# WKV recurrence on one core: a store piece issued by GpSimd from pair 42, VectorE rounding three of four k tiles, a ring of eleven, and new places in the order

## The chip, the core and the metric

The kernel runs on one core of a Trainium2 chip. Its engines work side by side, each in the order of its own queue: TensorE (PE, with its weight loads as PEld), VectorE (DVE), ScalarE (ACT), GpSimd (POOL) and SyncE (SP, which here only issues DMAs). The metric is the device time of one execution in microseconds (us). Differences within 0.3% are the ordinary spread of one kernel's runs.

## The reference

The inputs k and v are 16 batches of 2048 steps with 256 channels, float32; w and u have 256 channels. Per batch and channel a numerator, a denominator and their common exponent are carried along the 2048 steps:

```python
for t in range(seq_len):
    ww = u + kk
    qq = np.maximum(pp, ww)
    e1, e2 = np.exp(pp - qq), np.exp(ww - qq)
    output[b, t, :] = (e1 * aa + e2 * vv) / (e1 * bb + e2 + 1e-08)
    ww = pp - w + kk
    qq = np.maximum(ww, kk)
    e1, e2 = np.exp(ww - qq), np.exp(kk - qq)
    aa, bb, pp = e1 * aa + e2 * vv, e1 * bb + e2, qq
```

So the weight of an earlier step is the exponential of a running sum over k and w, and an output is a weighted sum of v over a sum of weights.

## The kernel before

**Tiling.** Time is cut into 16 chunks of 128 steps (time on the partitions), each of two halves of 64. A unit of work, called a pair here as in the words of the change, is n = 4c + p: chunk c of four batches, a tile of 128 x 1024. There are 64 pairs, with 512 KB of k, of v and of output each.

**One pair, front part.** `load_k` and `load_v` fetch k and v. TensorE needs k in a rounded float32 form. `how(n)` says who makes it: "C", the load converts while it moves the bytes, into the pool `kpool` (NK = 4 buffers); "D" or "P", the load is plain, into `kppool` (NKP = 1 buffer, tile `kf`), and `round_k` (L184) copies it on VectorE or GpSimd into a `kpool` buffer. From pair CF = 18 on the pattern PLAN "DCPC" is read by n modulo 4; before that it is "C", apart from the first BYSP = 1 pair, whose k and v are loaded by SP into `vpool` buffers and whose k VectorE rounds. All other loads are issued by GpSimd. Twice for each pair (q = 0 and 1), `rows` (R, four matmuls, L191) and `logs` (L, two matmuls, L197) build logarithms of weights in one of two PSUM tiles X, and `exps` (L200) exponentiates them on ScalarE into the ring EZR, which has RING = 12 slots. `cast_v` (CV, L204) makes v bfloat16, on VectorE for the first EARLY = 13 pairs and then on GpSimd, and `times_v` (TV, L209) multiplies it by the weights on VectorE. `sums` (S, L235) adds up halves on TensorE.

**One chunk, state.** After the last pair of a chunk a chain of small steps carries the state: CS (copy, VectorE), TU (turn, TensorE, L248), SL (logs, ScalarE), FR, OF (VectorE), SW (ScalarE), CH, SS (VectorE), TK (turn back, TensorE, L292) and BK (copy back, VectorE, L296).

**One pair, back part,** some LAG = 10 pairs later: DEN (twelve matmuls, L312, into an X tile), LN and INV on ScalarE (L320, L324: the reciprocal by logarithm and exponential, tile `rd`), NUM (twelve matmuls, L312, into the only `num` buffer), MUL (L332, VectorE, into one of NOT = 9 output tiles `ot`), and `store` (ST), a DMA for two batches and two half-size pieces for the other two. All three are issued by SP, but from pair BYPOOL = 52 on the third piece is issued by GpSimd.

**The order.** Nothing is moved at run time: each step has a place, a number in units of a pair (n plus an offset from the table P; for the back part n + LAG plus an offset; in the last ten pairs by the table TAIL). A list planner at the end takes, again and again, the step with the lowest place whose predecessors are taken and whose buffer is free by its count, and appends it to the program. Each engine then runs its own steps in that order and waits for data and buffers as they come.

**Fillers.** Before a step with a mode, the planner puts `zeros(m)`: m matmuls of zeros, 192 columns wide, into the PSUM tile TURN (L139). The number comes from P["Z0"] for pair or chunk 0 and from P["Z"] for all others; none are put between a TK and its BK, since both use TURN:

```python
        if o["mode"] and not quiet:
            zeros(P["Z0" if name[-1] < FILL else "Z"].get(name[0], 0))
        quiet = quiet and name[0] != "BK" or name[0] == "TK"
```

Before the change, Z has 3 zeros ahead of each TK and 5 ahead of each TU, none elsewhere.

Of the kernel before, what the change touches and what calls it, by code (L numbers as in the profile page):

```python
# [15 lines left out]
def kernel(  # L16
# [9 lines left out]
    K = tc.keep_in_program_order  # L26
    PE, DVE, SC, POOL, SP = nc.tensor, nc.vector, nc.scalar, nc.gpsimd, nc.sync

    B, T, Dm = k.shape
    HS = 64  # L30
    TC = 2 * HS
    NST = T // TC
    D = 2 * Dm
    NP = 4 * NST
    RING = 12
    LAG = 10.0
    BYSP = 1
    EARLY = 13
    PLAN = "DCPC"
    NK, NKP, NV, NVB, NRD, NOT = 4, 1, 5, 2, 2, 9  # L40
    RS = 2.0 ** -20
    CAP = 54.0
    BIG = 1e30
    CF = 18
    BYPOOL = 52
    FILL = 1
    P = {"LK": -3.78, "LV": -3.8, "RK": [-0.86, -0.8, -0.88, 0.32], "L": [-8.29, -9.105],
         "X": [-13.61, -10.365], "CV": [-1.2, -1.47, -0.325, -3.63], "TV": [-0.725, 2.11, 2.53, 2.655],
         "S": [3.82, -0.625, 3.55, -2.98], "wu": -1.11, "mats": -12.33,
         "STATE": [[-8.99, -10.35, -0.28, 1.3, -0.57, 0.74, -7.0, -3.75, 3.31, 8.1, 3.65, 2.26], [3.48, 0.85, -12.96, 4.2, -4.25, -19.41, 5.21, 2.49, 5.83, -18.64, -27.57, -14.52], [-4.09, -0.42, 5.79, 1.96, 4.88, 8.33, 12.29, 3.26, 16.8, 4.18, 4.62, 9.89]],  # L50
         "R": [-0.14, -5.32],
         "OUT": {"DEN": [0.405, 0.23, 0.63, 0.44], "LN": [-0.38, -1.93, -1.0, 0.545], "INV": [-19.65, -20.535, -21.555, -15.26], "NUM": [0.92, -10.27, -1.22, -3.96], "MUL": [2.175, 2.125, 1.96, 2.125], "ST": [-7.545, -4.04, -1.22, 5.625]},
         "TAIL": {"DEN": -3.02, "LN": -3.59, "INV": 2.66, "NUM": 1.08, "MUL": -6.56, "ST": 24.12, "step": 2.857},
         "Z0": {"L": 2, "S": 0, "DEN": 16, "NUM": 8, "TK": 32, "TU": 7, "R": 15},
         "Z": {"DEN": 0, "L": 0, "NUM": 0, "TK": 3, "S": 0, "TU": 5, "R": 0}}
# [21 lines left out]
    def matrix(name, dt):  # L77
        return consts.tile([128, 128], dt, tag=name, name=name)
# [24 lines left out]
    def load_v(n):  # L103
        vr = raw(vpool, "vr")
        K((SP if n < BYSP else POOL).dma_start(out=vr, in_=rows_of(v, n)))  # L105
        VR[n] = vr
# [15 lines left out]
    Z = consts.tile([128, 192], BF16, tag="Z", name="Z")  # L122
# [14 lines left out]
    def zeros(m, first=False):  # L137
        for j in range(m):
            K(PE.matmul(TURN[:, 0:192], Z[:, 0:128], Z, start=first, stop=True, skip_group_check=True))  # L139
# [28 lines left out]
    mats = {name: matrix(name, BF16) for name in ("Id", "IdN", "S", "SN")}  # L168
# [33 lines left out]
    def cast_v(n):  # L202
        vb = vbpool.tile([128, 4, Dm], BF16, tag="vb", name="vb")
        K((DVE if n < EARLY else POOL).tensor_copy(vb, VR.pop(n)))  # L204
        VB[n] = vb
# [94 lines left out]
    RD, NUM, OT = {}, {}, {}  # L300
# [29 lines left out]
    def mult(n):  # L330
        o = opool.tile([128, 4, Dm], F32, tag="ot", name="ot")
        K(DVE.tensor_mul(o.rearrange("p (i n) d -> p i (n d)", i=2), NUM.pop(n), RD.pop(n)))  # L332
# [12 lines left out]
    ops, free = {}, {"K": NK, "KP": NKP, "V": NV, "N": 1, "RD": NRD, "OT": NOT, "VB": NVB}
# [1 line left out]
    def step(name, place, fn, args=(), after=(), take=None, give=(), mode=0):  # L347
        ops[name] = dict(place=place, fn=fn, args=args, after=list(after), take=take, give=give, mode=mode)

    for n in range(NP):  # L350
        c, j = divmod(n, 4)
        early = n < BYSP
        put = lambda key: n + P[key][j]
        m = n + LAG
        tail = n >= NP - LAG
        place = lambda key: m + (P["TAIL"][key] + (n - NP + LAG) * P["TAIL"]["step"] if tail else P["OUT"][key][j])
        kb = "V" if early else "KP" if how(n) != "C" else "K"
        if n:
# [12 lines left out]
        step(("TV", n), put("TV"), times_v, (n,), [("X", 1, n), ("CV", n), ("TV", n - 1)], None, ["VB"])  # L371
        step(("S", n), put("S"), sums, (n,), [("TV", n), ("S", n - 1)] + ([("CS", c - 1)] if j == 0 else []), mode=2)
        if j == 3:
            s = P["STATE"][0 if c == 0 else 2 if c == NST - 1 else 1]
            for i, (name, fn, *after) in enumerate((
                    ("CS", copy_sums, ("S", n)), ("TU", turn, ("CS", c), ("CH", c - 1)), ("SL", state_logs, ("TU", c)),
                    ("FR", state_frames, ("SL", c), ("SN", c - 1)), ("OF", state_offsets, ("FR", c)),
                    ("SW", state_weights, ("OF", c)), ("CH", state_chain, ("SW", c), ("KP", c - 1)),
                    ("SS", state_spread, ("CH", c)), ("TK", turn_back, ("SS", c), "mats"), ("BK", copy_back, ("TK", c)),
                    ("SN", state_next, ("OF", c)), ("KP", state_keep, ("CH", c)))):  # L380
                if not (name in ("SN", "KP") and c + 1 == NST):
                    step((name, c), n + s[i], fn, (c,), after, mode=1)
# [70 lines left out]
```

## Time and profile before

| what | value |
|---|---|
| median of 3 runs | 302.77 us (302.64 to 303.08) |
| the profiled execution | 303.64 us, of which the span from first to last instruction is 301.9 us |
| mean granted TensorE clock | 0.991 of full speed |
| bytes moved by DMA | 101.21 MB, mean 335 GB/s |

The span is what the views of the profile show; 1.74 us of the profiled execution lie around it. "Busy" is the time in which an engine has an instruction at work; an instruction's start is recorded, the end of a matmul is modelled, so for TensorE the distance from start to start is read, not the busy time. In a timeline a line has the start, the length, the engine, the source line, the operation with output and input, and how many instructions of that kind follow each other (x4). In brackets stands the idle time of the engine before it, with what ended it.

### The profile page before, as it was taken

Reading aid. Unit: us, or ns where it says so; the run is one execution under the profiler, and the core shown is the slowest. Engines: PE = TensorE matmul, PEld = TensorE weight load, DVE = VectorE, ACT = ScalarE, POOL = GpSimd, SP = SyncE. Lnnn points to the kernel's source line nnn. Section 1 sums busy time; section 2 is a strip of 40 time slices with the busy share of each in tenths; the row PEclk is TensorE's granted clock in tenths of the full one; section 3 lists DMA queues with packets and bytes.
Section 4 is the critical chain, followed back from the end, with each engine's and each line's share of the span. In section 5 each row is a group of like instructions: output and inputs, shape, how many; then the busy total and the mean of one; then the engine's idle time right before and its main releaser. Section 6 shows DMA issues by size and latency. Waiting matters only on the chain.

```text
span 301.9 us, 7960 instructions
## 1 busy us (share of the span) xinstructions
PE 279.1 (92%) x3194; PEld 140.6 (47%) x3194; DVE 238.5 (79%) x395; ACT 260.2 (86%) x289; POOL 172.7 (57%) x217
## 2 busy tenths in 40 slices
PE   7989989999999999999899999999899999996851
PEld 7536444444544454544445454445345444443420
DVE  6466865978889888977988888887988878978752
ACT  1585678999999999999899999999799997995990
POOL 8464452739577376857657576857666485521321
PEclk9999999999999999999999999999999999999996
DMA  7999999999999999999999999999999999964786
GB/s 177 339 344 348 347 350 347 329 366 314 373 375 367 374 378 353 382 377 372 347 371 371 371 380 379 382 378 370 353 357 370 372 367 346 340 172 128 229 242 171
DMA packets 69302, 101.21 MB, mean 335 GB/s; under 512 B 5128, under 2 KB 57872, under 8 KB 69264
## 3 DMA queue, kind: packets, MB, share of 16 engines
q0 software_dynamic: 34080, 67.64, 73.5%
q1 hardware_dynamic: 35168, 33.04, 35.3%
q8 instruction: 25, 0.41, 0.6%
q14 instruction: 13, 0.11, 0.1%
q10 hardware_dynamic: 16, 0.01, 0.0%
HBM read 67.12 MB, written 33.55 MB: 333 GB/s over the span
## 4 chain that ended last, share of the span: by engine, by line
PE 33%; DMA 31%; issue 13%; POOL 12%; DVE 7%; ACT 2%; POOLq 0%; DVEq 0%
DMA kf<-in_k_dram 26%; PE X L197 9%; PE num L312 6%; PE TURN L139 5%; PE X L312 5%; PE X L191 5%; DMA vr<-in_v_dram 4%; POOL kr L184 3%; DVE ot L332 3%; POOL vr L105 3%; DVE kr L184 2%; POOL kr L101 2%; PE TOT L235 2%; POOL vb L204 1%; PE TOT L248 1%
## 5 line engine op out<-in xcount | busy, mean ns | idle before, releaser
L200 ACT ACTIVATE EZR<-X 128x1024 bf16<-128x1024 f32 x128 | 124.2, 1015 | 12.5 <-PE X L197 12.5
L209 DVE TENSOR_TENSOR EZR<-EZR,vb 128x2048 bf16<-128x2048 bf16 x64 | 91.3, 1443 | 12.8 <-POOL vb L204 10.8
L332 DVE TENSOR_TENSOR ot<-num,rd 128x1024 f32<-128x1024 f32 x64 | 77.8, 1215 | 10.0 <-PE X L312 3.1
L204 POOL CAST vb<-vr 128x1024 bf16<-128x1024 f32 x51 | 53.8, 1076 | 40.4 <-DVE EZR L209 38.7
L320 ACT ACTIVATE rd<-X 128x1024 f32<-128x1024 f32 x64 | 65.4, 1022 | 5.8 <-PE X L312 2.1
L324 ACT ACTIVATE rd<-rd 128x1024 f32<-128x1024 f32 x64 | 67.8, 1059 | 2.0
L191 PE MATMUL X<-WU,CO 64*64 64x512 bf16 x512 | 52.5, 399 | 0.7
L105 POOL DMA_DIRECT2D vr<-in_v_dram x63 | 48.5, 769 | 1.5 <-issue 1.0
L197 PE MATMUL X<-kr,NLE 128*128 128x512 f32 x128 | 46.9, 448 | 0.8 <-DMA kr<-in_k_dram 0.8
L197 PE MATMUL X<-kr,NLZ 128*128 128x512 f32 x128 | 46.8, 447 | 0.0
L101 POOL DMA_DIRECT2D kr<-in_k_dram x40 | 30.5, 763 | 25.7 <-PE X L197 25.7
L312 PE MATMUL num<-EZR,SN 64*64 64x512 bf16 x256 | 26.2, 398 | 11.4 <-DVE ot L332 11.3
L191 PEld LDWEIGHTS <-CO 64*64 64x64 bf16 x512 | 15.5, 103 | 34.6 <-issue 31.1
L139 PE MATMUL TURN<-Z 128*128 128x192 bf16 x250 | 29.3, 262 | 1.6 <-DVE Z L123 1.6
L139 PEld LDWEIGHTS <-Z 128*128 128x128 bf16 x250 | 20.8, 104 | 15.5 <-issue 13.6
L312 PE MATMUL X<-EZR,S 64*64 64x512 bf16 x256 | 25.4, 380 | 0.9 <-ACT EZR L200 0.5
L197 PEld LDWEIGHTS X<-kr,NLE 128*128 128x128 f32 x128 | 19.0, 188 | 15.3 <-issue 12.9
L197 PEld LDWEIGHTS X<-kr,NLZ 128*128 128x128 f32 x128 | 19.0, 188 | 14.3 <-issue 14.3
L98 POOL DMA_DIRECT2D kf<-in_k_dram x23 | 17.5, 759 | 14.4 <-DVE U L257 9.3
L312 PE MATMUL X<-cb,Id 64*64 64x512 bf16 x256 | 25.3, 376 | 0.0
L312 PE MATMUL X<-EZR,Id 64*64 64x512 bf16 x256 | 25.3, 376 | 0.0
L312 PE MATMUL num<-cb,IdN 64*64 64x512 bf16 x256 | 25.1, 376 | 0.0
(63 smaller groups left out, 259.5 us busy)
## 6 DMA issues: line engine op xcount, KB each, us to landing
vr<-in_v_dram POOLq DMA_DIRECT2D x63, 512.0 KB, 9.5
kr<-in_k_dram POOLq DMA_DIRECT2D x40, 512.0 KB, 9.6
out_dram<-ot SPq DMA_DIRECT2D x64, 256.0 KB, 6.8
out_dram<-ot SPq DMA_DIRECT2D x116, 128.0 KB, 7.5
kf<-in_k_dram POOLq DMA_DIRECT2D x23, 512.0 KB, 6.9
out_dram<-ot POOLq DMA_DIRECT2D x12, 128.0 KB, 3.0
vr<-in_k_dram SPq DMA_DIRECT2D x1, 512.0 KB, 4.3
vr<-in_v_dram SPq DMA_DIRECT2D x1, 512.0 KB, 5.3
```

The source lines that it names most:

```text
L101: K(POOL.dma_start(out=KR[n], in_=rows_of(k, n)))
L105: K((SP if n < BYSP else POOL).dma_start(out=vr, in_=rows_of(v, n)))
L139: K(PE.matmul(TURN[:, 0:192], Z[:, 0:128], Z, start=first, stop=True, skip_group_check=True))
L191: K(PE.matmul(X[a][o:o + HS, i, :].rearrange("p (n d) -> p n d", n=2), CO[r:r + HS, q, :], WU[r:r + HS, :].unsqueeze(1).broadcast_to([HS, ...
L197: K(PE.matmul(X[a][:, i, :], (NLE, NLZ)[q], km[:, i, :], start=False, stop=True, skip_group_check=True))
L200: K(SC.activation(ez(n)[:, q, 1], X[a], ACT.Exp))
L204: K((DVE if n < EARLY else POOL).tensor_copy(vb, VR.pop(n)))
L209: K(DVE.tensor_mul(ez(n)[:, :, 0], ez(n)[:, :, 1], vb.unsqueeze(1).broadcast_to([128, 2, 2, D])))
L312: K(PE.matmul(out_tile[o:o + HS, i, :], left, right, start=s == 0, stop=s == 2, tile_position=(r, o), skip_group_check=True))
L320: K(SC.activation(rd, X[a], ACT.Ln, scale=RS))
L324: K(SC.activation(RD[n], RD[n], ACT.Exp, scale=-1.0))
L332: K(DVE.tensor_mul(o.rearrange("p (i n) d -> p i (n d)", i=2), NUM.pop(n), RD.pop(n)))
```

## The change

It changes several numbers and one function. RING 12 to 11; NKP 1 to 4 and NOT 9 to 8; BYSP 1 to 5 (the k and v of five pairs are loaded by SP, all into `vpool`, and VectorE rounds their k); EARLY 13 to 9; from pair CF = 11 on the pattern is "CDDD", so one of four k is converted by its load and three are rounded by VectorE, none by GpSimd. The third piece of a store becomes a step of its own, SQ, issued by GpSimd where `shared(n)` holds. With BYQ "PPPP", BYF = 42 and BYPOOL = 52 this is from pair 42 on (the words given with the change say 34; the code says 42). The output tile then comes free, by the planner's count, at SQ. All places are new, and so are the fillers: one zero ahead of every L, 6 ahead of TK, 7 ahead of TU. SOON = 0 makes `lead` zero, so the two terms with it change nothing.

```diff
-    RING = 12
+    RING = 11
     LAG = 10.0
-    BYSP = 1
-    EARLY = 13
-    PLAN = "DCPC"
-    NK, NKP, NV, NVB, NRD, NOT = 4, 1, 5, 2, 2, 9
+    SOON = 0
+    UNTIL = 32
+    SHARE = 0.8
+    BYSP = 5
+    EARLY = 9
+    PLAN = "CDDD"
+    NK, NKP, NV, NVB, NRD, NOT = 4, 4, 5, 2, 2, 8
...
-    CF = 18
+    CF = 11
     BYPOOL = 52
+    BYQ = "PPPP"
+    BYF = 42
...
-         "R": [-0.14, -5.32],
-         "OUT": {"DEN": [0.405, 0.23, 0.63, 0.44], "LN": [-0.38, -1.93, -1.0, 0.545], "INV": [-19.65, -20.535, -21.555, -15.26], "NUM": [0.92, -10.27, -1.22, -3.96], "MUL": [2.175, 2.125, 1.96, 2.125], "ST": [-7.545, -4.04, -1.22, 5.625]},
-         "TAIL": {"DEN": -3.02, "LN": -3.59, "INV": 2.66, "NUM": 1.08, "MUL": -6.56, "ST": 24.12, "step": 2.857},
-         "Z0": {"L": 2, "S": 0, "DEN": 16, "NUM": 8, "TK": 32, "TU": 7, "R": 15},
-         "Z": {"DEN": 0, "L": 0, "NUM": 0, "TK": 3, "S": 0, "TU": 5, "R": 0}}
+    P = {"LK": -4.23, "LV": -3.05, "RK": [-6.215, -1.065, -4.64, -1.435], "L": [-11.915, -4.075],
...
+         "STATE": [[-7.03, 2.76, -4.48, 2.96, -1.67, 3.61, -5.96, -3.62, -6.62, 6.55, 5.21, 2.79], [2.47, -0.56, -12.38, 3.54, -15.96, -12.68, 4.6, -0.33, 4.8, -5.0, -36.92, -24.78], [-3.38, -1.58, 3.78, 3.8, 8.32, 12.18, 9.51, 9.1, 19.04, 19.02, 7.77, 12.4]],
+         "R": [-0.705, -6.055],
+         "OUT": {"DEN": [-0.315, -0.12, -0.115, -0.435], "LN": [-12.435, -10.725, -2.26, -7.46], "INV": [-16.945, -9.17, -7.565, -5.25], "NUM": [0.135, -1.195, 0.095, -4.985], "MUL": [1.27, 0.765, 0.83, 0.505], "ST": [-4.815, 3.81, -2.455, 6.34], "SQ": [-5.51, 7.465, -2.71, 8.45]},
+         "TAIL": {"DEN": -5.11, "LN": -13.85, "INV": 0.42, "NUM": -0.16, "MUL": -4.06, "ST": 16.44, "step": 3.818, "SQ": 24.64},
+         "Z0": {"L": 7, "S": 0, "DEN": 0, "NUM": 3, "TK": 53, "TU": 0, "R": 5},
+         "Z": {"DEN": 0, "L": 1, "NUM": 0, "TK": 6, "S": 0, "TU": 7, "R": 0}}
...
+    def piece(n, h, queue):
+        c, p = divmod(n, 4)
+        t0 = c * TC + HS * (1 - h)
+        K(queue.dma_start(out=out[4 * p + 2:4 * p + 4, t0:t0 + HS, :].rearrange("n t d -> t n d"), in_=OT[n][HS * h:HS * h + HS, 2:4, :]))
+
+    def shared(n):
+        return n >= BYPOOL or BYQ[n % len(BYQ)] == "P" and n >= BYF
+
     def store(n):
         c, p = divmod(n, 4)
-        o = OT.pop(n)
-        K(SP.dma_start(out=out[4 * p:4 * p + 2, c * TC:(c + 1) * TC, :].rearrange("n t d -> t n d"), in_=o[:, 0:2, :]))
-        for h in range(2):
-            t0 = c * TC + HS * (1 - h)
-            K((POOL if h and n >= BYPOOL else SP).dma_start(
-                out=out[4 * p + 2:4 * p + 4, t0:t0 + HS, :].rearrange("n t d -> t n d"), in_=o[HS * h:HS * h + HS, 2:4, :]))
+        K(SP.dma_start(out=out[4 * p:4 * p + 2, c * TC:(c + 1) * TC, :].rearrange("n t d -> t n d"), in_=OT[n][:, 0:2, :]))
+        for h in range(1 if shared(n) else 2):
+            piece(n, h, SP)
+
+    def store_rest(n):
+        piece(n, 1, POOL)
...
-        m = n + LAG
+        lead = SOON * max(0.0, 1 - n / UNTIL)
+        m = n + LAG - lead
...
-        step(("ST", n), place("ST"), store, (n,), [("MUL", n), ("ST", n - 1)], None, ["OT"])
+        step(("ST", n), place("ST"), store, (n,), [("MUL", n), ("ST", n - 1)], None, [] if shared(n) else ["OT"])
+        if shared(n):
+            step(("SQ", n), place("SQ"), store_rest, (n,), [("ST", n)], None, ["OT"])
```

More of the change, by code (lines that the diff above doesn't have):

```diff
@@ L43 @@
     BIG = 1e30
-    CF = 18
+    CF = 11
     BYPOOL = 52
+    BYQ = "PPPP"
+    BYF = 42
     FILL = 1
[L47 to L50, printed above, removed]
-         "R": [-0.14, -5.32],
-         "OUT": {"DEN": [0.405, 0.23, 0.63, 0.44], "LN": [-0.38, -1.93, -1.0, 0.545], "INV": [-19.65, -20.535, -21.555, -15.26], "NUM": [0.92, -10.27, -1.22, -3.96], "MUL": [2.175, 2.125, 1.96, 2.125], "ST": [-7.545, -4.04, -1.22, 5.625]},
-         "TAIL": {"DEN": -3.02, "LN": -3.59, "INV": 2.66, "NUM": 1.08, "MUL": -6.56, "ST": 24.12, "step": 2.857},
-         "Z0": {"L": 2, "S": 0, "DEN": 16, "NUM": 8, "TK": 32, "TU": 7, "R": 15},
-         "Z": {"DEN": 0, "L": 0, "NUM": 0, "TK": 3, "S": 0, "TU": 5, "R": 0}}
+    P = {"LK": -4.23, "LV": -3.05, "RK": [-6.215, -1.065, -4.64, -1.435], "L": [-11.915, -4.075],
+         "X": [-10.925, -3.815], "CV": [0.85, -2.6, -0.655, -7.835], "TV": [-2.23, 1.825, 1.285, 1.395],
+         "S": [2.865, -2.42, 2.115, -1.83], "wu": -9.4, "mats": -10.67,
+         "STATE": [[-7.03, 2.76, -4.48, 2.96, -1.67, 3.61, -5.96, -3.62, -6.62, 6.55, 5.21, 2.79], [2.47, -0.56, -12.38, 3.54, -15.96, -12.68, 4.6, -0.33, 4.8, -5.0, -36.92, -24.78], [-3.38, -1.58, 3.78, 3.8, 8.32, 12.18, 9.51, 9.1, 19.04, 19.02, 7.77, 12.4]],
[4 more added lines that the diff above has]
+         "Z": {"DEN": 0, "L": 1, "NUM": 0, "TK": 6, "S": 0, "TU": 7, "R": 0}}
     consts = ctx.enter_context(tc.tile_pool(name="consts", bufs=1))
@@ L381 @@
                 if not (name in ("SN", "KP") and c + 1 == NST):
-                    step((name, c), n + s[i], fn, (c,), after, mode=1)
+                    step((name, c), n + s[i] - lead * SHARE, fn, (c,), after, mode=1)
         step(("DEN", n), place("DEN"), den, (n,), [("BK", c), ("DEN", n - 1), "mats"], "X", mode=3)
```

## The prediction, made before the changed kernel ran

> **What bounds the kernel now.** I read the page first, then the busy times by stage, cut at the second LN (48.27 us) and at the LN of pair 53 (267.8 us).
>
> ```profile
> DMA  7999999999999999999999999999999999964786
> 0.00:48.27 48.27, 44.41 (x399) 26.83 (x403) 30.33 (x80) 28.59 (x31) 26.00 (x46) 1.00 1.31 319
> 48.27:267.80 219.53, 214.92 (x2500) 103.92 (x2496) 187.01 (x286) 208.84 (x235) 139.40 (x159) 1.00 1.12 362
> 267.80:301.90 34.10, 19.73 (x307) 9.81 (x299) 21.18 (x31) 22.76 (x24) 7.28 (x12) 0.92 0.66 186
> ```
>
> The columns of a stage are its length, then busy time of PE, PEld, DVE, ACT and POOL, the granted clock, the DMA share and GB/s. The DMA row of the page is at 9 nearly everywhere and misleads: bytes move at 362 GB/s where each pair needs 1.5 MB per 4.2 us, so they follow the pair rate. In the middle PE is busy for 214.9 and ACT for 208.8 of 219.5 us, at full clock. Which of the two sets the pace is seen in the timeline (PE, ACT and one VectorE line, from one chunk's round):
>
> ```profile
> 61.04 0.41 PE L191 MATMUL X<-WU,CO 64*64 64x512 bf16 x4
> 66.61 1.92 ACT L200 ACTIVATE EZR<-X 128x1024 bf16<-128x1024 f32 x2
> 68.44 0.42 PE L139 MATMUL TURN<-Z 128*128 128x192 bf16 x3
> 68.56 1.03 ACT L320 ACTIVATE rd<-X 128x1024 f32<-128x1024 f32 x1
> 68.70 0.39 PE L292 MATMUL TURN<-Id,CB 128*128 128x128 bf16 x4
> 69.12 0.69 DVE L296 CAST cb<-TURN 128x512 bf16<-128x512 f32 x1 [1.36 <-PE TURN L292]
> 72.44 0.62 PE L235 MATMUL TOT<-EZR,OH 128*32 128x256 bf16 x16
> 72.56 1.03 ACT L320 ACTIVATE rd<-X 128x1024 f32<-128x1024 f32 x1
> 76.42 0.59 PE L139 MATMUL TURN<-Z 128*128 128x192 bf16 x5
> 76.53 1.03 ACT L320 ACTIVATE rd<-X 128x1024 f32<-128x1024 f32 x1
> 76.84 0.61 PE L248 MATMUL TOT<-Sel,ts 128*128 128x96 f32 x4
> 77.38 0.41 PE L191 MATMUL X<-WU,CO 64*64 64x512 bf16 x4
> ```
>
> The instruction that stands behind DEN on PE starts at 68.44, 72.44, 76.42, and LN follows it by 0.12, 0.12, 0.11: LN starts as DEN ends. The two exps that stand ahead of it on ACT end at 68.53 (66.61 + 1.92), almost the same moment. So ACT waits for PE, by less than 0.1 a pair: PE paces, ACT is close behind. A chunk (four pairs) from R to R takes 77.38 - 61.04 = 16.34 us, of which the fillers are 68.70 - 68.44 = 0.26 for three and 76.84 - 76.42 = 0.42 for five, 0.085 each. The middle holds 52 pairs, LN 1 to 52:
>
> ```profile
> 48.27:267.80 219.53, 53.16 (x52) 1.00 1.12 362
> ```
>
> Thirteen chunks at 16.34 are 212.4; the other 7.1 us are stalls. The single `kf` buffer is my main suspect: its loop of load and rounding is the longest line of the chain of waits and GpSimd waits for it:
>
> ```profile
> DMA kf<-in_k_dram 26%; PE X L197 9%; PE num L312 6%; PE TURN L139 5%; PE X L312 5%; PE X L191 5%; DMA vr<-in_v_dram 4%; POOL kr L184 3%; DVE ot L332 3%; POOL vr L105 3%; DVE kr L184 2%; POOL kr L101 2%; PE TOT L235 2%; POOL vb L204 1%; PE TOT L248 1%
> POOL kr L184 <- DMA kf<-in_k_dram: 15.2, 10, 2.5
> ```
>
> **The middle: the fillers.** TK goes from 3 to 6 and TU from 5 to 7: five more a chunk, 5 x 0.085 = 0.43 us. One zero ahead of each L is eight a chunk. The trace has two zeros in that place, for pair 0 alone, and for pair 1 the place without them:
>
> ```profile
> 8.38 0.41 PE L191 MATMUL X<-WU,CO 64*64 64x512 bf16 x4
> 8.91 0.74 PE L197 MATMUL X<-kr,NLE 128*128 128x512 f32 x2
> 10.83 0.41 PE L191 MATMUL X<-WU,CO 64*64 64x512 bf16 x4
> 11.29 0.71 PE L197 MATMUL X<-kr,NLZ 128*128 128x512 f32 x2
> 11.93 0.41 PE L191 MATMUL X<-WU,CO 64*64 64x512 bf16 x4
> 12.27 0.73 PE L197 MATMUL X<-kr,NLE 128*128 128x512 f32 x2
> ```
>
> From R to L it is 0.53 and 0.46 with two zeros and 0.34 without, so 0.06 to 0.095 a zero; I take 0.07, eight are 0.56 (0.48 to 0.76). Nothing hides this: PE paces, and ACT's slack is under 0.1 a pair. A clock that rises is no return, it is 1.00 here. The chunk becomes 16.34 + 0.43 + 0.56 = 17.33; places of S (n + 2.865, -2.42, 2.115, -1.83) now take the four S in three goes rather than two, one more change of kind of matmul, estimated at 0.07 (0 to 0.15; the nearest row is the 0.34 from R to L, which holds such a change and four matmuls). So 17.4 (17.25 to 17.7), times 13 = 226.2, which is 13.8 over the 212.4.
>
> A zero behind BK must also wait until VectorE has read TURN. By places TK (4c + 7.8) and BK come together, and PE then has DEN (7.885) and NUM (8.095), 24 matmuls, ahead of the next R and L, while BK's copy takes 0.69 (69.12 above): hidden. With only R's 0.34 as cover it would cost some 0.4 a chunk.
>
> **The middle: buffers, rounding and GpSimd.**
>
> ```profile
> L209 DVE TENSOR_TENSOR EZR<-EZR,vb 128x2048 bf16<-128x2048 bf16 x64 | 91.3, 1443 | 12.8 <-POOL vb L204 10.8
> L184 POOL CAST kr<-kf 128x1024 fp32r<-128x1024 f32 x12 | 14.1, 1177 | 16.3 <-DMA kf<-in_k_dram 15.2 <-PE X L197 1.0
> L184 DVE CAST kr<-kf 128x1024 fp32r<-128x1024 f32 x11 | 7.5, 682 | 0.7 <-DMA kf<-in_k_dram 0.5
> 175.73 2.05 POOL L204 CAST vb<-vr 128x1024 bf16<-128x1024 f32 x2
> 176.84 2.03 DVE L209 TENSOR_TENSOR EZR<-EZR,vb 128x2048 bf16<-128x2048 bf16 x1 [0.70 <-POOL vb L204]
> 184.23 1.22 DVE L209 TENSOR_TENSOR EZR<-EZR,vb 128x2048 bf16<-128x2048 bf16 x1
> ```
>
> Four `kf` buffers end the loop of one; I take back 5 of the 7.1 us. GpSimd loses 12 roundings (14.1 us) and the issue of 8 loads, and gains four casts (1.03 each) and the issue of ten pieces: it stays near its 139 of 219 us, and hidden. VectorE rounds 45 k tiles rather than 12; 28 of the 33 more fall into the middle (the first five lie in the head, where it has time), 28 x 0.68 = 19 us on 187, so 206 of 226: hidden under PE with 20 us to spare, where it has 32 now. MUL gets less room: NUM (n) was placed behind the logs of the next pair, now right behind DEN, so LN and INV (2.1 us) run after NUM instead of beside the next logs, and the one `num` buffer is held longer. I put new stalls at 2 (0 to 6). The middle: 219.5 - 5 + 13.8, with 2.1 of the old stalls left being these 2: **+8.7 us** (+4.6 to +14).
>
> The Trainium skill (SBUF — State Buffer, Who interferes with whom) says VectorE and GpSimd share a port pair under an exclusive lock: a two-port VectorE cast, or one with two SBUF inputs against a reading GpSimd, blocks the other engine wholly. The trace agrees in part: L209 takes 2.03 us beside a GpSimd cast and 1.22 alone. By it the 12 lost GpSimd roundings would give VectorE up to 12 x 0.8 = 10 us back, and PE would still set the same sum.
>
> **The head.**
>
> ```profile
> 9.68 1.02 ACT L200 ACTIVATE EZR<-X 128x1024 bf16<-128x1024 f32 x1 [5.49 <-PE X L197]
> 27.87 2.81 PE L139 MATMUL TURN<-Z 128*128 128x192 bf16 x32
> 43.68 1.50 PE L139 MATMUL TURN<-Z 128*128 128x192 bf16 x16
> 45.88 0.83 PE L139 MATMUL TURN<-Z 128*128 128x192 bf16 x8
> 46.00 1.02 ACT L320 ACTIVATE rd<-X 128x1024 f32<-128x1024 f32 x1 [1.10 <-PE X L312]
> ```
>
> The fillers ahead of DEN and NUM of pair 0 (16 and 8, here right in front of LN 0 and LN 1) become 0 and 3: 21 x 0.085 = -1.8. Those ahead of TK of chunk 0 become 53: 21 x 0.085 = +1.8, counted in full though PE there also waits for loads. BK of chunk 0 moves from place 11.1 to 9.55, so DEN 0 comes behind the logs of pair 10 rather than 11, and LN and INV of pair 0 (2.1 us) fall into time in which ACT waits (it is busy for 28.6 of 48.3 us): -2.1. SP issues five tiles at the start where it issued two; the first exps waited 5.49 us up to 9.68, and the places of rounding k and of the row for w and u come ahead of CV now: -1.3 (0 to -2). Together **-3.4** (-6, if the 53 fillers hide under loads and SP brings 2; -1, if the arrival of k and v sets LN 1 anyway).
>
> **The tail.**
>
> ```profile
> 288.92 1.22 DVE L332 TENSOR_TENSOR ot<-num,rd 128x1024 f32<-128x1024 f32 x1 [1.00 <-DMA out_dram<-ot]
> 291.14 1.22 DVE L332 TENSOR_TENSOR ot<-num,rd 128x1024 f32<-128x1024 f32 x1 [1.00 <-PE num L312]
> out_dram<-ot POOLq DMA_DIRECT2D x12, 128.0 KB, 3.0
> DMA to landing us min/median/max: 2.4/7.4/9.6
> ```
>
> The last outputs come every 291.14 - 288.92 = 2.22 us, the loop of the one `num` buffer, NUM then MUL, which stays. MUL 51 moves from 0.24 behind R of pair 63 (63.125 and 62.86) to 0.79 ahead of it (61.505 and 62.295): about one pair less remains at the end. I take -1.5 (0 to -2.2). Against it stands a new wait: with eight output tiles MUL 51 writes where pair 43 was, whose third piece, SQ 43, has place 61.45, right ahead of MUL 51 at 61.505. GpSimd comes to it behind SQ 50 (which waits for MUL 50) and a cast, an estimated 3 us into the 4.2 us between the two MULs; with a landing of 3.0 (the same queue, last loads done) MUL 51 waits 1.8, with 7.4 it waits 6. I take +1.5 (0 to +6): behind it on VectorE stand TV and all later MULs, for which NUM, the stores and the tail wait. SQ of pairs 42 to 53 with even numbers come right behind their MUL and hold GpSimd's loads up to that MUL; with loads four places ahead of use (-4.23, -3.05) that is hidden. The tail: **0** (-2 to +5).
>
> **The sum.** -3.4 + 8.7 + 0 = +5.3 on the profiled execution's 303.64 us gives 308.9. That execution lies 0.87 above the median of the runs, so I predict **308.0**; its own range, by the terms' bounds taken not all at one end, is 303 to 313.
>
> **Rivals.**
>
> *The fillers cost nothing* (faster). If something else than PE holds each L (ACT, an X tile), the zeros fall into waits, and the middle is 13 x 16.3 plus 2 = 214: -5.5 - 3.4 gives 303.64 - 8.9 - 0.87 = 293.9. For it speaks that ACT is busy for 208.8 us, so close behind; against it, that LN starts with the end of DEN in three of three rows.
>
> *The gains win* (faster). The fillers cost their lower bound (17.25 x 13 = 224.3), no stall remains (+4.8), the head brings 6 and the tail 2: -3.2, 299.6. For it: 7.1 us of stalls and 20 us of idle ACT in the head are there to be won. Against it: every term must fall on the good side.
>
> *VectorE becomes the bound* (slower still). It is idle for 32.5 us of the middle now, in waits that its order imposes (10.8 of them for GpSimd's casts, and waits for TK as at 69.12). If they all stay, 206 + 32.5 = 238.5 sets the middle, +19 - 3.4: 318.4. It decides once its waits pass the 20 us that PE leaves it. Against it: MUL 4c - 3 now stands between CH and TK (7.765 against 7.6 and 7.8), which fills one of them.
>
> *The late pieces* (slower still). If SQ lands in 7 to 10 us, MUL 51, and behind it MUL 53 and 55 (over SQ 45 and 47), wait 6, 2 and 2 us: some +8 more, 316. Against it: 3.0 us for that queue.
>
> That the words say 34 and the code 42 makes no rival: eight more issues on GpSimd would be hidden as those are.
>
> **How the numbers follow.** Forecast 0.53, free fillers 0.12, gains 0.16, VectorE 0.12, late pieces 0.07. Faster by over 0.2% (what runs of this kernel can tell from no change): 0.28, the second and third. Within 0.2%: 0.03, from the lower end of the forecast. Slower: 0.69. The range of 299.5 to 314.5 takes in the third case and most of the forecast and leaves out the second and the upper part of the last two.
>
> **What would show it.** Right: a chunk from R to R takes about 17.4 us in undisturbed stretches and LN still starts with the end of DEN; some 270 zeros in the middle (13 + 8 a chunk) where there were 104; LN 1 near 45 us; no waits for `kf`; MUL 51 waiting for a store. Wrong: a chunk at 16.3 to 16.6 in spite of the zeros (fillers free); L waiting for k, or NUM waiting for MUL in most pairs (VectorE paces); LN 1 later than 48.

## The result, and the profile after

The changed kernel takes 298.21 us (298.15 to 298.56, four runs) against 302.92 (302.64 to 303.3): the ratio is 0.9846, with a 95% interval of 0.9829 to 0.9863. It is 4.7 us faster where 5.2 slower was forecast. The profiled execution takes 298.19 us with a span of 296.5.

The busy times by stage of the changed kernel, cut at the same events as before the change (start of LN 1 and of LN 53; columns: length, then PE, PEld, DVE, ACT and POOL busy, granted clock, DMA share, GB/s), and the fillers (L144) in the middle:

```profile
0.00:46.40 46.40, 42.64 (x413) 25.44 (x417) 33.26 (x83) 28.63 (x32) 23.46 (x41) 1.00 1.14 324
46.40:262.57 216.17, 215.51 (x2669) 111.80 (x2665) 197.26 (x313) 208.78 (x235) 133.25 (x156) 1.00 1.05 366
262.57:296.50 33.93, 19.66 (x299) 10.81 (x298) 19.89 (x30) 22.65 (x25) 9.46 (x16) 0.88 0.73 206
46.40:262.57 216.17, 45.15 (x273) 22.57 (x273) 1.00 1.05 366
```

| stage | before | after | difference | forecast |
|---|---|---|---|---|
| head, to LN 1 | 48.27 | 46.40 | -1.9 | -3.4 |
| middle, LN 1 to LN 53 | 219.55 | 216.17 | -3.4 | +8.7 |
| tail, to the end of the span | 34.10 | 33.93 | -0.2 | 0 |

The stages are those of one execution each, so they add up to 5.4 and not to 4.7. The forecast failed in the middle, by 12 us. The 52 pairs of the middle are 13 chunks; their lengths, worked out as the distance from every fourth start of LN to the next, tell more than the mean:

| kernel | chunks of the middle, us | middle |
|---|---|---|
| before | 16.31 16.35 16.35 17.1 16.33 17.99 16.76 16.6 16.38 18.32 16.77 17.97 16.31 | 219.55 |
| after | 16.68, then eleven of 16.55 to 16.57, 17.33 | 216.17 |

Before, undisturbed chunks of 16.3 stand beside disturbed ones of 16.6 to 18.3. After, all chunks but the first and the last are equal, a little longer than the best ones before. The chain of waits of the page says the same: it ran over loads of `kf` before, and is mostly TensorE now.

```profile
PE 78%; issue 8%; DVE 4%; ACT 4%; POOL 3%; DMA 2%; POOLq 0%; DVEq 0%; ACTq 0%
```

One chunk of the changed kernel in the timeline, from R to R (each line: start, length, engine, line, operation):

```profile
60.41 0.41 PE L196 MATMUL X<-WU,CO 64*64 64x512 bf16 x4
60.76 0.26 PE L144 MATMUL TURN<-Z 128*128 128x192 bf16 x1
60.80 0.71 PE L202 MATMUL X<-kr,NLZ 128*128 128x512 f32 x2
61.43 0.62 PE L240 MATMUL TOT<-EZR,OH 128*32 128x256 bf16 x16
62.07 0.41 PE L317 MATMUL X<-EZR,S 64*64 64x512 bf16 x4
63.36 0.41 PE L196 MATMUL X<-WU,CO 64*64 64x512 bf16 x4
...
76.98 0.41 PE L196 MATMUL X<-WU,CO 64*64 64x512 bf16 x4
```

The chunk is 76.98 - 60.41 = 16.57 us. From R to L it is 60.80 - 60.41 = 0.39 with the filler, where 0.34 was measured without: not 0.07 more, but 0.05, and the logs that follow take 61.43 - 60.80 = 0.63 where they took 0.66. DEN and NUM together, with R behind them, take 63.36 - 62.07 = 1.29.

### The profile page after: what moved, and what is told of

It is laid out like the page before. It is cut to its first block, busy times and chain, and to the rows that moved or that the text cites. A ratio compares the mean times of both kernels' runs of the same rounds, so it can differ in the third digit from the quotient of the medians.

```text
span 296.5 us, 8281 instructions
## 1 busy us (share of the span) xinstructions
PE 277.8 (94%) x3370; PEld 148.0 (50%) x3370; DVE 250.4 (84%) x424; ACT 260.1 (88%) x289; POOL 166.2 (56%) x211
## 4 chain that ended last, share of the span: by engine, by line
PE 78%; issue 8%; DVE 4%; ACT 4%; POOL 3%; DMA 2%; POOLq 0%; DVEq 0%; ACTq 0%
PE X L202 19%; PE X L317 13%; PE TURN L144 13%; PE X L196 12%; PE num L317 11%; PE TOT L240 6%; POOL out_dram L343 3%; ACT EZR L205 2%; PE TOT L253 2%; DMA WUf<-in_u_dram 2%; DVE EZR L214 1%; PE TURN L297 1%; ACT rd L329 1%; ACT rd L325 1%; DVE AB L283 0%
## 5 line engine op out<-in xcount | busy, mean ns | idle before, releaser
L205 ACT ACTIVATE EZR<-X 128x1024 bf16<-128x1024 f32 x128 | 125.6, 1014 | 14.8 <-PE X L202 14.3
L209 POOL CAST vb<-vr 128x1024 bf16<-128x1024 f32 x55 | 59.8, 1087 | 87.8 <-DVE EZR L214 83.9
L214 DVE TENSOR_TENSOR EZR<-EZR,vb 128x2048 bf16<-128x2048 bf16 x64 | 77.7, 1215 | 3.0 <-ACT EZR L205 2.9
L144 PE MATMUL TURN<-Z 128*128 128x192 bf16 x426 | 63.6, 255 | 1.6 <-DVE Z L128 1.6
L144 PEld LDWEIGHTS <-Z 128*128 128x128 bf16 x426 | 36.3, 100 | 45.9 <-issue 44.1
L110 POOL DMA_DIRECT2D vr<-in_v_dram x59 | 44.9, 762 | 1.0 <-DVE CB L290 1.0
L103 POOL DMA_DIRECT2D kf<-in_k_dram x40 | 33.8, 844 | 0.5 <-DMA kr<-in_k_dram 0.5
L196 PEld LDWEIGHTS <-CO 64*64 64x64 bf16 x512 | 15.4, 104 | 34.1 <-issue 30.3
L189 DVE CAST kr<-kf 128x1024 fp32r<-128x1024 f32 x40 | 26.3, 685 | 0.0
L317 PE MATMUL num<-EZR,IdN 64*64 64x512 bf16 x256 | 25.6, 378 | 0.0
L343 POOL DMA_DIRECT2D out_dram<-ot x22 | 13.3, 607 | 19.2 <-DVE ot L337 12.7
```

Of the source, the lines that this page charges most:

```text
L196: K(PE.matmul(X[a][o:o + HS, i, :].rearrange("p (n d) -> p n d", n=2), CO[r:r + HS, q, :], WU[r:r + HS, :].unsqueeze(1).broadcast_to([HS, ...
L205: K(SC.activation(ez(n)[:, q, 1], X[a], ACT.Exp))
L214: K(DVE.tensor_mul(ez(n)[:, :, 0], ez(n)[:, :, 1], vb.unsqueeze(1).broadcast_to([128, 2, 2, D])))
L317: K(PE.matmul(out_tile[o:o + HS, i, :], left, right, start=s == 0, stop=s == 2, tile_position=(r, o), skip_group_check=True))
```

## The experiments

All kernels ran beside runs of the kernel before; times are medians, with the interval of the ratio to the kernel before in brackets. Where two experiments are compared with each other or with the changed kernel, it is by their own times, whose ranges are under 1 us if none is given.

**1. What does the filler ahead of L cost?** The changed kernel without it:

```diff
-         "Z": {"DEN": 0, "L": 1, "NUM": 0, "TK": 6, "S": 0, "TU": 7, "R": 0}}
+         "Z": {"DEN": 0, "L": 0, "NUM": 0, "TK": 6, "S": 0, "TU": 7, "R": 0}}
```

> The changed kernel without the zero ahead of each L. Theory A (the prediction's price, 0.07 us for each of 104 zeros in the middle, on the engine that paces): 298.2 - 7.3, though no lower than ScalarE's own pace allows, so 291 to 293.5. Theory B (a zero between R and L falls into a change of matmul kind that is paid anyway): 298.2 within 0.6, and from R to L 0.34 us without it against 0.38 with it.

Measured: 296.17 us (296.07 to 296.63; 0.979, 0.972 to 0.985), 2.0 less than the changed kernel. The chunks are 16.43 to 16.55, but for the last of 17.32. So the 126 fillers outside pair 0 cost 0.016 us each. The time lies between the two theories, and the price of one filler far nearer to B's.

**2. The same filler in the kernel before**, and nothing else:

```diff
-         "Z": {"DEN": 0, "L": 0, "NUM": 0, "TK": 3, "S": 0, "TU": 5, "R": 0}}
+         "Z": {"DEN": 0, "L": 1, "NUM": 0, "TK": 3, "S": 0, "TU": 5, "R": 0}}
```

> The kernel before with one zero ahead of each L and nothing else. Theory A: 302.9 + 7.3 in the middle and up to 1.5 in the head, 310 to 312. Theory B: 302.9 to 303.8, a chunk from R to R at 16.34 to 16.5 us.

Measured: 304.78 us (304.19 to 306.06; 1.008, 1.005 to 1.011). All chunks are 16.94 to 17.01: 0.66 longer than the undisturbed ones before, which is near theory A's length, though not for A's reason, as will be seen. Yet the middle is only 220.9 against 219.55, since no chunk is longer than that any more. (The tail adds 1.2 us; the granted clock is 0.66 there from 274 to 279 us.) The timeline of this kernel, around TK, shows where the 0.66 comes from:

```profile
103.15 0.39 PE L292 MATMUL TURN<-Id,CB 128*128 128x128 bf16 x4
103.47 0.41 PE L191 MATMUL X<-WU,CO 64*64 64x512 bf16 x4
104.32 0.24 PE L139 MATMUL TURN<-Z 128*128 128x192 bf16 x1 [0.44 <-DVE cb L296]
104.34 0.72 PE L197 MATMUL X<-kr,NLE 128*128 128x512 f32 x2
104.99 0.41 PE L191 MATMUL X<-WU,CO 64*64 64x512 bf16 x4
105.33 0.26 PE L139 MATMUL TURN<-Z 128*128 128x192 bf16 x1
105.37 0.71 PE L197 MATMUL X<-kr,NLZ 128*128 128x512 f32 x2
```

The first filler behind TK waits until VectorE has copied TURN (BK): R to L is 104.34 - 103.47 = 0.87 instead of 0.38, half a microsecond a chunk. The other seven share the remaining 0.16, 0.02 each. In the old order R follows TK at once; in the changed order DEN and NUM stand between, as the prediction had it, and the wait is hidden. And a chunk of 17.0 has no stalls on top, which suggests that whatever makes the stalls of the kernel before has a period of its own, near that length.

**3. All fillers of the middle taken out**, in the changed kernel and in the kernel before:

```diff
-         "Z": {"DEN": 0, "L": 1, "NUM": 0, "TK": 6, "S": 0, "TU": 7, "R": 0}}
+         "Z": {"DEN": 0, "L": 0, "NUM": 0, "TK": 0, "S": 0, "TU": 0, "R": 0}}
...
-         "Z": {"DEN": 0, "L": 0, "NUM": 0, "TK": 3, "S": 0, "TU": 5, "R": 0}}
+         "Z": {"DEN": 0, "L": 0, "NUM": 0, "TK": 0, "S": 0, "TU": 0, "R": 0}}
```

> The changed kernel with no filler at all outside chunk 0 (L, TK and TU at zero). If TensorE paces (13 fillers ahead of TK and TU at 0.085 are 1.1 us of a chunk's 16.57): the chunk falls until ScalarE sets it, to 16.1 to 16.3 us, 292 to 295. If ScalarE or VectorE already sets 16.57: 298.2 within 0.6. If the fillers hold the clock up: a granted clock below 1.00 in the middle and over 299.

> The kernel before without its eight fillers a chunk (TK and TU at zero). TensorE paces the undisturbed stretches: chunk 16.34 down to ScalarE's 16.1 to 16.2, so -2 to -3, 300 to 301. If the kf loop (load and rounding through one buffer) is what sets the mean of 16.9: no change, 302.9 within 0.6, the stalls take up what the fillers leave.

Measured: 295.81 us (295.48 to 297.33; 0.978, 0.972 to 0.984) and 303.48 us (301.06 to 304.6; 1.000, 0.996 to 1.004). In the changed kernel the chunk goes from 16.56 to 16.45, not to 16.1, though 21 fillers a chunk are gone; the granted clock of the middle stays at 1.00. TensorE is busy for 10.1 us less there than with the fillers (205.39 instead of 215.51), but the middle is only 1.8 us shorter. The rest has become waits of TensorE, 8.7 us by the two lines below, where with the fillers there is one wait of 0.45 (the middle's busy times, then its waits: engine, what waited, for what, us in total, times, longest):

```profile
45.81:260.18 214.37, 205.39 (x2396) 98.90 (x2392) 196.94 (x313) 208.39 (x235) 131.46 (x155) 1.00 1.06 369
PE TURN L297 <- DVE CB L290: 6.3, 12, 1.3
PE X L317 <- ACT EZR L205: 2.4, 13, 0.2
```

In the kernel before the undisturbed chunks fall to 16.13 to 16.17 and the disturbed ones are 16.3 to 17.7. The time is the same, but that is a sum of two things. The middle is 217.2 us, 2.3 less than before, as thirteen chunks shorter by 0.18 would have it; its 7.1 us of stalls stay, so they don't take up what the fillers leave. The tail is 37.5 us instead of 34.1, for there the granted clock falls, where it was 1.00 from 267.82 to 285 us before:

```profile
264.83:272.00 7.17, 4.65 (x68) 1.66 (x67) 5.91 (x10) 5.09 (x6) 1.25 (x2) 0.89 0.34 101
272.00:282.00 10.00, 7.84 (x96) 3.92 (x92) 6.12 (x13) 6.48 (x8) 1.81 (x3) 0.74 0.51 144
```

So a faster TensorE does shorten the old order's middle, and the fillers of its last chunks seem to pay by holding the clock. No run takes out the fillers of the tail alone.

**4. The kf loop.** The kernel before with a second `kf` buffer (one output tile is given up for its room):

```diff
-    NK, NKP, NV, NVB, NRD, NOT = 4, 1, 5, 2, 2, 9
+    NK, NKP, NV, NVB, NRD, NOT = 4, 2, 5, 2, 2, 8
```

> The kernel before with two kf buffers instead of one, and eight output tiles instead of nine to make room. Theory K (the loop load, round, load again through one kf buffer takes 8.4 us for each second pair, 16.8 a chunk, and makes the stalls): every chunk near 16.35 us, no long ones, 13 x 16.35 + 1 in the middle, 302.8 - 6 = 296 to 298. Rival O (the stalls come from the order or from GpSimd's roundings): chunks of 17 to 18 us stay, 302 to 303.5.

Measured: 295.64 us (295.19 to 296.49; 0.978, 0.975 to 0.981). All chunks are 16.31 to 16.36. The busy times of its middle:

```profile
47.24:259.75 212.51, 212.51 (x2501) 101.81 (x2497) 181.43 (x286) 208.90 (x235) 147.29 (x159) 1.00 1.12 370
```

The middle is 212.5 us, 13 x 16.35, without any stall. The second buffer alone gives 7.1 us, more than the whole change. The order, the GpSimd roundings and the fillers are those of the kernel before, so rival O falls: the single buffer is what these stalls hang on.

Two more kernels bear on it: the kernel before with PLAN "CCCC", so that no plain load and no rounding is left from pair 18 on, and the changed kernel with NKP back at 1:

```diff
-    PLAN = "DCPC"
+    PLAN = "CCCC"
...
-    NK, NKP, NV, NVB, NRD, NOT = 4, 4, 5, 2, 2, 8
+    NK, NKP, NV, NVB, NRD, NOT = 4, 1, 5, 2, 2, 8
```

> The kernel before with all k of pairs 18 to 63 converted by their loads, so no kf tile, no rounding on VectorE or GpSimd from there on. Theory K: no loop, no stalls, 296 to 298. If converting loads are themselves slow or their buffers (four kr, held until the logs) are too few: waits of the logs for kr, 303 or more.

> The changed kernel with one kf buffer instead of four. Theory K: three loads a chunk go through one buffer, each 6.5 to 8 us to land and 1 us to round, so a chunk takes 22 to 26 us from pair 11 on and the kernel 370 to 420 us. Rival O: 298 to 305.

Measured: 303.7 us (303.33 to 306.07; 1.005, 1.002 to 1.007) and 386.04 us (385.25 to 388.21; 1.278, 1.271 to 1.285). The second is what theory K asks for. Its waits (engine, what waited, for what, then us in total, times, longest):

```profile
POOL kf L103 <- DVE kr L189: 136.5, 31, 5.8
```

GpSimd holds the next load until VectorE has rounded from the only buffer. The first missed: from the seventh chunk of the middle on they are 16.8 to 18.5 us long, with no `kf` at all. Its waits:

```profile
POOL kr L101 <- PE X L197: 81.0, 47, 5.4
PEld X L197 <- DMA kr<-in_k_dram: 14.2, 26, 1.7
```

With all k converted by their loads, the four `kr` buffers are all there is: each is held from the issue of its load to the logs that read it, and its load lands 12.6 us after the issue (median of the page). GpSimd waits for the logs, the logs wait for the load. So the wider statement is: four buffers for k, or four and one, are too few for this pace, and four and two are enough in the old order. The loads of `kr` also take longer than before the change (12.6 against 9.6), and no run separates that from the number of buffers. That the `kf` loop was the place where it showed in the kernel before is theory K; that it is the only such place is not so.

**5. The roundings taken from GpSimd.** The changed kernel with the old pattern:

```diff
-    PLAN = "CDDD"
+    PLAN = "DCPC"
```

> The changed kernel with the old pattern DCPC (one of four k rounded by GpSimd, two converted) and four kf buffers. Theory K: no stalls, chunk 16.5 to 16.6, 298.2 within 1. Rival O (taking the rounding from GpSimd ended the stalls): VectorE's products take up to 2 us beside GpSimd's roundings again and the middle grows by 3 us or more, 301 to 303.

Measured: 440.24 us (439.11 to 441.74; 1.456, 1.450 to 1.462), which tells nothing about GpSimd's roundings. VectorE waits for loads of `kf` 110 us in 13 waits, and GpSimd waits as long for `kr` buffers that TensorE still reads. That the changed places put roundings ahead of loads that come late is the likely reading. The pattern and the places can't be swapped apart here. About GpSimd's roundings the kernel with the second buffer says more: it keeps them, and all its chunks are as short as the undisturbed ones, so they make no stall there.

**6. The fillers of chunk 0.** The changed kernel without those ahead of TK:

```diff
-         "Z0": {"L": 7, "S": 0, "DEN": 0, "NUM": 3, "TK": 53, "TU": 0, "R": 5},
+         "Z0": {"L": 7, "S": 0, "DEN": 0, "NUM": 3, "TK": 0, "TU": 0, "R": 5},
```

> The changed kernel without the 53 fillers ahead of TK of chunk 0. If the 4.87 us in which ScalarE waits for the logs at 30 to 35 us come from these fillers: LN 1 at 42 to 43.5 us instead of 46.4, so 294.5 to 296. If the loads set the head (k and v arrive at some 345 GB/s whatever TensorE does): LN 1 at 45.5 to 46.4 and 297.5 to 298.2.

Measured: 298.89 us (0.986, 0.984 to 0.988), 0.7 more than the changed kernel, with LN 1 at 47.67, 1.3 us later. Neither of the two was expected. The timeline of this kernel at TK of chunk 0, and its busy times by stage around it (the last three columns are granted clock, DMA share, GB/s):

```profile
31.70 0.61 PE L297 MATMUL TURN<-Id,CB 128*128 128x128 bf16 x4 [2.70 <-DVE CB L290]
33.49 0.64 PE L196 MATMUL X<-WU,CO 64*64 64x512 bf16 x4
34.06 1.22 PE L202 MATMUL X<-kr,NLE 128*128 128x512 f32 x2
35.21 0.64 PE L196 MATMUL X<-WU,CO 64*64 64x512 bf16 x4
```

```profile
28.50:31.70 3.20, 0.50 (x3) 0.06 (x1) 2.24 (x11) 1.82 (x3) 3.20 (x5) 0.90 1.46 346
31.70:37.00 5.30, 5.29 (x36) 2.10 (x40) 4.88 (x7) 1.03 (x1) 1.50 (x3) 0.50 1.25 351
```

TK waits 2.70 us for VectorE anyway. It then runs 1.5 us earlier than behind 53 fillers (31.70 against 33.19), but at a clock of 0.50: R to L takes 0.57 and the logs 1.15, for 5.3 us, which loses more than was won. With the fillers the clock is 1.00 from 28.5 to 38 us: there they hold it.

**7. The pieces on GpSimd.** The changed kernel with GpSimd issuing pieces from pair 52 on only (BYPOOL), as before the change:

```diff
-    BYF = 42
+    BYF = 64
```

> The changed kernel with its store pieces on GpSimd from pair 52 only, as before the change, and not from 42. The prediction's view (hidden, but for the wait of MUL 51 for the late piece of pair 43, which the trace of the changed kernel doesn't show): 298.2 within 0.6. A rival, that the ten pieces on GpSimd relieve SP's queue: 299 or more.

Measured: 296.82 us (0.979, 0.977 to 0.981): 1.4 less than the changed kernel, so the pieces from pair 42 on cost time. The last full chunk is 16.74 instead of 17.33. VectorE and GpSimd of the changed kernel there, then of this one:

```profile
245.20 1.22 POOL L343 DMA_DIRECT2D out_dram<-ot  x2
245.91 1.33 DVE L283 TENSOR_TENSOR_SCAN AB<-G,TB 128x96 f32<-128x96 f32 x2
247.20 1.05 POOL L209 CAST vb<-vr 128x1024 bf16<-128x1024 f32 x1
247.27 1.05 DVE L293 COPY TB<-AB 128x64 f32<-128x64 f32 x1
248.61 0.40 PE L297 MATMUL TURN<-Id,CB 128*128 128x128 bf16 x4 [0.45 <-DVE CB L290]
```

```profile
246.11 1.56 DVE L283 TENSOR_TENSOR_SCAN AB<-G,TB 128x96 f32<-128x96 f32 x2
246.15 1.05 POOL L209 CAST vb<-vr 128x1024 bf16<-128x1024 f32 x1
247.71 0.21 DVE L293 COPY TB<-AB 128x64 f32<-128x64 f32 x1
```

Two pieces (1.22 us) push GpSimd's cast from 246.15 to 247.20, off the scans (1.33 instead of 1.56) and upon the small copy of the state, which takes 1.05 instead of 0.21; TK then waits 0.45 for the step behind it. Another 0.95 us lie behind LN 63 (285.62 to the end of the span is 10.85, against 9.90 in the kernel of this experiment). There MUL 63 starts 2.59 behind MUL 62 instead of 2.22, in a stretch with a granted clock of 0.77 (285.6 to 290.3 us), where the kernel of this experiment has 1.00. That the pieces cause this isn't shown: two kernels above that have them too (experiments 1 and 3) take 10.6 and 10.5 us there, with MUL 63 at 2.22.

**8. Better versions.** The kernel before with two `kf` buffers and no fillers in the middle, then without those of chunk 0 too:

```diff
-    NK, NKP, NV, NVB, NRD, NOT = 4, 1, 5, 2, 2, 9
+    NK, NKP, NV, NVB, NRD, NOT = 4, 2, 5, 2, 2, 8
-         "Z": {"DEN": 0, "L": 0, "NUM": 0, "TK": 3, "S": 0, "TU": 5, "R": 0}}
+         "Z": {"DEN": 0, "L": 0, "NUM": 0, "TK": 0, "S": 0, "TU": 0, "R": 0}}
...
-         "Z0": {"L": 2, "S": 0, "DEN": 16, "NUM": 8, "TK": 32, "TU": 7, "R": 15},
+         "Z0": {"L": 2, "S": 0, "DEN": 0, "NUM": 0, "TK": 0, "TU": 0, "R": 15},
```

> The kernel before with two kf buffers, eight output tiles and no fillers outside chunk 0. With the kf loop gone the fillers are on the path: chunk 16.35 down to the 16.15 that the kernel before without fillers showed in its undisturbed chunks, 13 x 0.2 = -2.6, 293. If stalls come back at the faster pace: 295 to 296.

> The same, and chunk 0 without its fillers ahead of TK, TU, DEN and NUM too (32, 7, 16 and 8). If these stand on the way to LN 1: 63 x 0.085 = -5 at most, LN 1 at 42 to 45 instead of 47.2, 288 to 291. If the loads set the head: LN 1 at 46.5 or later, 292.5 to 293.

Measured: 296.02 us (293.91 to 297.21; 0.976, 0.973 to 0.979) and 297.41 us (297.32 to 299.26; 0.983, 0.980 to 0.985). The first has chunks of 16.13 to 16.18 up to a last one of 16.58, as expected, but its runs differ by 3 us and it is not told apart from the one with fillers. Here too the middle is 2.0 us shorter (210.6 against 212.5) and the tail 2.7 longer (36.4 against 33.7), at a granted clock of 0.86 from 258.05 to 265.2 and 0.76 in the next 10 us. The second has one chunk of 19.9 us at 232 to 246 us, in which the granted clock falls to 0.88; ahead of it MUL waits 1.79 us for a store to leave its output tile, and NUM then 1.57 for MUL. Whether a ninth output tile would prevent that was not run. LN 1 stays at 47.26, so the 63 fillers of chunk 0 were not on the way to it; that the loads are is likely, not shown.

**9. Where NUM stands.** The kernel before with two `kf` buffers, no fillers in the middle, and NUM behind its own DEN:

```diff
-"NUM": [0.92, -10.27, -1.22, -3.96], "MUL": [2.175, 2.125, 1.96, 2.125]
+"NUM": [0.41, 0.24, 0.64, 0.45], "MUL": [1.2, 1.2, 1.2, 1.2]
```

> The kernel before with two kf buffers, no fillers outside chunk 0, and NUM of a pair placed right behind its own DEN (MUL follows), as the change has it. If this place makes the difference: DEN and NUM together take 1.3 us instead of 1.42 where R follows, but a chunk is 16.4 to 16.5 us, as LN now starts 0.22 behind the last matmuls of DEN and ScalarE waits after TU; 296 + 13 x 0.3 = 299 to 300. If not: chunk 16.15, 295 to 296.

Measured: 313.78 us (312.61 to 315.68; 1.032, 1.027 to 1.037), chunks of 17.27 to 17.38, longer than expected. In its timeline:

```profile
105.40 0.73 PE L197 MATMUL X<-kr,NLZ 128*128 128x512 f32 x2
106.76 0.41 PE L312 MATMUL X<-EZR,S 64*64 64x512 bf16 x4 [0.64 <-ACT EZR L200]
```

DEN follows the logs at once and waits for ScalarE to leave its X tile; in the old order NUM of the pair before stands between them. In the changed order S, or fillers and TK, or fillers and TU stand between the logs and DEN of each pair (in the chunk shown above, S at 61.43). The changed kernel without fillers has a trace of the same wait:

```profile
106.29 0.41 PE L317 MATMUL X<-EZR,S 64*64 64x512 bf16 x4 [0.18 <-ACT EZR L205]
```

**10. All that was found to cost taken out of the changed kernel**:

```diff
-    BYF = 42
+    BYF = 64
-         "Z": {"DEN": 0, "L": 1, "NUM": 0, "TK": 6, "S": 0, "TU": 7, "R": 0}}
+         "Z": {"DEN": 0, "L": 0, "NUM": 0, "TK": 0, "S": 0, "TU": 0, "R": 0}}
```

> The changed kernel without fillers outside chunk 0 and with the pieces on GpSimd only from pair 52. If the two costs add (2.4 us and 1.4 us): 294.2 to 294.8. If they are the same wait seen twice: 295.5 to 296.

Measured: 294.39 us (294.09 to 294.99; 0.970, 0.967 to 0.973), the fastest of all by its median. The costs add. What is left of the change, buffers, head and order, is 8.7 us faster than the kernel before that ran beside it, and some 1.2 faster than the second buffer alone. The new order isn't what wins: its middle is 213.8 us against 212.5 with the old order and the second buffer, its LN 1 comes at 46.08 instead of 47.24.

## Why the prediction was wrong

**What bounds the kernel: half right.** TensorE sets the undisturbed chunk of the old order and ScalarE is close behind; the kernel before without fillers (16.34 to 16.16) agrees. In the changed order TensorE is busy nearly all the time too, but in part with fillers that stand in waits (experiment 3). And it did not set the mean. 7.1 us of stalls were seen and the one `kf` buffer was named as the suspect; 5 were taken back. All 7.1 went with a second buffer, and in the changed kernel 216.17 - 13 x 16.56 = 0.9 is left, most of it in the last chunk: -6.2, where -5 was forecast.

**The fillers and the order: this step failed.** "Nothing hides this: PE paces" was put at 13.8 us over thirteen chunks of 16.34. The chunk grew by 0.23 instead of 1.06, 3.0 us in all. Three things were wrong:

- The filler ahead of L was put at 0.07 by two fillers in pair 0. By the distances, the first of two falls into the change from R's kind of matmul to L's, and only the second costs its 0.085. By the trace it is 0.02 and by the kernel without it 0.016.
- The order was given +0.07 for S. S does cost more (three goes, some 0.2 a chunk by start-to-start distances), but behind DEN and NUM now stands R, which is of their kind: the two take 1.29 to 1.32 instead of 1.42, three times a chunk, -0.3.
- The stretches of fillers ahead of TK and TU grew by 0.26 and 0.16 as computed, and yet all 21 fillers of a chunk cost 0.11 (16.56 against 16.45 without). In part they now stand right behind the logs, which are full 128 x 128 matmuls as they are: from the last logs to the next start it is 0.55 (97.89 to 98.44), where in the old order NUM followed after 0.66, -0.2 a chunk. For the most part they stand in waits, which the trace without them shows.

Ahead of TK in the changed kernel, then in the one without fillers:

```profile
97.89 0.71 PE L202 MATMUL X<-kr,NLZ 128*128 128x512 f32 x2
98.44 0.67 PE L144 MATMUL TURN<-Z 128*128 128x192 bf16 x6
98.95 0.39 PE L297 MATMUL TURN<-Id,CB 128*128 128x128 bf16 x4
```

```profile
96.55 0.73 PE L202 MATMUL X<-kr,NLZ 128*128 128x512 f32 x2
97.74 0.40 PE L297 MATMUL TURN<-Id,CB 128*128 128x128 bf16 x4 [0.46 <-DVE CB L290]
```

TK waits for `CB`, which VectorE makes from the state: 6.3 us in the middle. DEN waits for the exps, as in experiment 9: 2.4 us. Together they are the 8.7 us of experiment 3. One thing that makes `CB` late: in every chunk of the middle one of the two scans of the state takes 1.08 us, 0.73 more than the usual 0.35 (shortest, median and longest of 32, in ns, before and after):

```profile
L278 DVE TENSOR_TENSOR_SCAN AB<-G,TB x32: 330/346/358, 28.9 to 281.6; 128x96 f32<-128x96 f32 x32
L283 DVE TENSOR_TENSOR_SCAN AB<-G,TB x32: 323/345/1082, 30.6 to 274.8; 128x96 f32<-128x96 f32 x32
```

In the chunk shown, GpSimd issues three loads in a row at that time (96.17 to 98.41). But before the change scans run beside issues of loads without being stretched, so what holds the scan is left open, and so is whether the wait of TK would go with it.

The rival "the fillers cost nothing" was therefore near the truth with 0.12. Its reason was half right: fillers do fall into waits, but the waits are those of TK and DEN, and not of L; and its 293.9 counted on a chunk of 16.3. The rival that came nearest in time, "the gains win" at 299.6, was 1.4 off by luck: it counted on a chunk of 17.25, 6 us from the head and 2 from the tail, where 16.56, 1.9 and 0.2 were measured.

**Rounding on VectorE and GpSimd's share: right.** VectorE is busy for 197 us of the middle instead of 206 computed, as TV is no longer stretched (1215 ns in the mean, 1443 before), and MUL waits for ScalarE, not for room. With the fillers in place TensorE waits for VectorE once, 0.45 us, so the rival of VectorE as the bound fell; without them it is VectorE's `CB` that TK waits for.

**The head: -1.9 instead of -3.4, and most terms not borne out.** LN 0 moved from 46.00 to 42.03, LN 1 only from 48.27 to 46.40. The -1.8 for the fillers ahead of DEN and NUM shows in no run: in the old order the 63 fillers of chunk 0, those 24 among them, change LN 1 by 0.2 (47.49 to 47.26, experiment 8). The -2.1 for the earlier BK would fit, but nothing shows it by itself. SP's five tiles made the first exps later, not earlier:

```profile
7.90 0.29 DVE L170 CAST WU<-WUf 128x256 bf16<-128x256 f32 x1 [2.31 <-DMA WUf<-in_u_dram]
10.39 1.02 ACT L205 ACTIVATE EZR<-X 128x1024 bf16<-128x1024 f32 x1 [6.21 <-PE X L202]
```

The small row of u, issued by ScalarE at 2.36, arrives 5.45 us later by the chain of waits, while the five tiles load (that they delay it wasn't tested alone); the first exps start at 10.39 instead of 9.68, where -1.3 was forecast. The 53 fillers, charged with 1.8, cost nothing: without them LN 1 comes 1.3 us later.

**The tail: the sum right by luck, with a wait that doesn't exist.** MUL 51 was said to wait for the piece of pair 43. It starts at 256.26 while GpSimd issues that piece at 255.93 or later, earlier than any piece lands (2.3 us at least), and it waits for ScalarE alone. So the output buffer it writes must be another one: the buffers weren't handed out in turn here, as the step took for granted. The forecast of 0 was -1.5 for the earlier MUL 51 and +1.5 for that wait. With the pieces on GpSimd only from pair 52 the tail is 33.0, 1.1 less than before, and with those from 42 on 33.9, for a reason that was not forecast and is in part open (experiment 7).

## What to carry to other kernels

Look at the distribution of the period before its mean: equal undisturbed periods with long ones between them point to a second loop, and a longer period of the bounding engine may then vanish in the stalls (0.66 more in each of 13 chunks, 8.6 us, cost 1.4 in the middle). Where nothing changes in sum, look at the stages: without its fillers the kernel before won 2.3 us in the middle and lost 3.4 in the tail, where the granted clock fell. Count, for each kind of load, buffers times pace against the time from issue to the last reader, and add the buffer before anything else: one of 512 KB gave 7.1 us, more than a new order of everything. A busy engine isn't a pacing one if part of its work is filler: take the filler out and see which waits come up. The price of an extra instruction on the pacing engine is read at the very place where it goes, one of it and not two, since the first may fall into a gap that is paid already.

## What the hardware showed

TensorE's granted clock fell to 0.50 after a wait of 2.70 us (0.90 in the stage of the wait, 0.50 in the 5.3 us behind it) and matmuls took twice as long for that time; 53 matmuls of zeros in the same wait kept it at 1.00. The Trainium skill (TensorE: Matmul & The Clock Gate, Part 1: The HAM clock gate) gives the same two rates, and puts the idle time that is needed at about 3.4 us; the wait seen here is shorter. In the tail of the kernel before without fillers it fell behind waits of 0.82 and 1.70 us (0.89 and 0.74 in the two stages of experiment 3), while behind one of 1.88 in chunk 0 of the last kernel of experiment 8 it stayed at 1.00 (28 to 36 us). So the length of one wait alone doesn't decide.

A VectorE copy of 128 x 64 took 1.05 us beside a GpSimd cast of 1.05, five times its 0.21. The Trainium skill (SBUF — State Buffer, Who interferes with whom) says that a copy in a two-port mode and GpSimd lock each other out, and whoever comes second waits until the first is done. Here the copy ends 0.07 us behind the cast, less than its own 0.21, so the trace agrees in the main only.
